# Two factors of the normalised input, T3 and T4, summed by accumulating transfers inside SBUF instead of VectorE

## The chip, the core and the metric
The kernel runs on one core of one Trainium2 chip. The metric is the device time of one launch in microseconds (us), as the median of several runs. The engines are TensorE (PE; its weight loads are PEld), VectorE (DVE), ScalarE (ACT), GpSimd (POOL) and SyncE (SP). SP and POOL also start transfers: SP through hardware queues, POOL through a software queue, which alone is used here for transfers that add to what lies at their target.

## The reference
A decoder trunk of two layers on 512 tokens of width 1024. Each layer is a gated feed-forward, a mixer, and a second gated feed-forward:

```
x = x + 0.5 * swiglu(rms_norm(x, ffn1_norm[l]), ffn1_w_gate[l], ffn1_w_up[l], ffn1_w_down[l])
x = x + mixer_l(rms_norm(x, mix_norm[l]))
x = x + 0.5 * swiglu(rms_norm(x, ffn2_norm[l]), ffn2_w_gate[l], ffn2_w_up[l], ffn2_w_down[l])

def rms_norm(x, g):
    y = x * rsqrt(mean(x * x, axis=-1) + 1e-6)
    return y * g
def swiglu(x, w_gate, w_up, w_down):
    return (silu(x @ w_gate) * (x @ w_up)) @ w_down
```
All inputs are float32; the hidden width is 2816.

## The kernel before, in words
`x` stays in SBUF, as eight tiles of 128 features by 512 tokens. The feed-forward `ffn` is called four times: first and second feed-forward of both layers, with a mixer between the first and the second call and another between the third and the fourth. Its matrix products use a scheme of seven products for a 2x2 block product. The normalised input is cut into four blocks: b11 and b12 are the first 512 features for the first and the last 256 tokens, b21 and b22 the same of the last 512 features. Its right factors are

- B11 = b11, B21 = b21, N22 = -b22,
- T1 = b12 - b11, N2 = T1 - b22, T3 = b22 - b12, T4 = b11 - b21 + T3 (written before as -(N2) - b21).

Every factor and every weight chunk is split into a high part, by a cast on ScalarE (L87), and a residue, by a subtraction on VectorE (L88); each product then takes three matmuls (high by high, high by residue, residue by high). The order of the products is fixed by hand (`staggered`): P5 and P1 of the first unit, then P6, P2, P7, then P5 of the next unit, P3, P1 of the next, P4. Their right factors are P5: T1, P1: B11, P6: N2, P2: B21, P7: T3, P3: N22, P4: T4.

A call begins with a stage of its own. The first pair of gate and up columns is computed from the input before its norm is known, by four `quarter`s of 24 matmuls of 512 columns each; the norm's sums (`norm`) are put in among them. While TensorE works on these, the normalised blocks `xn` are made on VectorE (L379) and the seven factors are built from them in the order of the code: B11, T1, N2, B21, T3, N22, T4. T1, N2 and T4 are made one after the other in the half `t1` of a tile `hz`, T3 in its other half `t3`. There is one buffer for `hz`: the next hidden tile of that name is first written at L460 and has to wait until everything in the old one has been read. The quarters' four PSUM banks are read at L455 and L458 (a product with R), L456 (SiLU on ScalarE) and L460 to L464. The PSUM pool has six banks: four for the quarters, two for X and Y of the first unit, so P2's bank Z comes free when a quarter's bank has been read. P1 and then P6, P7 and P4 write bank X in turn: P6 waits until ScalarE has copied P1's result away (`x1`, L482), P7 until it has copied P6's (`x2`, L482).

Weight chunks come by SP's transfers into `sto`, `ar` and `a`; the sums of weights that the scheme needs are made by accumulating transfers that POOL starts (L124). A scheduler sets each engine's order when the kernel is built, from the order of the code and the dependences; an engine works through its own list in order.

Of the kernel before, what the change touches and what calls it, by code (L numbers as in the profile page):

```python
# [13 lines left out]
ALU = mybir.AluOpType  # L14
# [27 lines left out]
def trunk(ctx: ExitStack, tc: tile.TileContext, a, out):  # L42
# [12 lines left out]
    nc = tc.nc  # L55
# [8 lines left out]
    def bank(tag="bank", bufs=None):  # L64
        return pp.tile([P, 512], F32, tag=tag, name=tag, bufs=bufs)
# [20 lines left out]
    def split(raw, hi, lo):  # L86
        nc.scalar.copy(hi, raw)  # L87
        nc.vector.tensor_sub(lo, raw, hi.bitcast(F32))  # L88
# [22 lines left out]
    class Seven(Chunk):  # L111
# [11 lines left out]
        def add(self, tag, q):  # L123
            nc.gpsimd.dma_start(out=self.unit[tag], in_=self.srcs[q], accum_op=ALU.add)  # L124
# [42 lines left out]
    for l in range(2):  # L167
        for f in ("ffn1", "ffn2"):
# [21 lines left out]
            for kind, p in what:  # L190
                if kind == "gu":
                    units.append(seven([gu[p, q] for q in range(4)], CH, turn))
                else:
                    gi, e = p
# [11 lines left out]
    def weights(ahead=3, fetched=6):  # L206
        i = used[0]
        used[0] += 1
        while len(ready) < min(i + ahead, len(chunks)):
            while (loaded[0] < min(max(len(ready) + 1, i + fetched), len(chunks))  # L210
                   and chunks[loaded[0]].turn <= now[0]):
                chunks[loaded[0]].load()
                loaded[0] += 1
            ready.append(chunks[len(ready)].halves())
        return ready[i]

    def mm3(ps, wh, wl, ah, al, start, stop):
        nc.tensor.matmul(ps, wh, ah, start=start, stop=False)  # L218
        nc.tensor.matmul(ps, wh, al, start=False, stop=False)  # L219
        nc.tensor.matmul(ps, wl, ah, start=False, stop=stop)  # L220
# [98 lines left out]
    def norm_columns():  # L319
        ps = held()  # L320
        for sq in Norm.late:
            nc.vector.tensor_add(Norm.acc, Norm.acc, sq)
        Norm.late.clear()
        token_sums(ps, Norm.acc)
        v = sp.tile([P, NT], F32, tag="nv", name="nv")
        nc.vector.tensor_scalar(v, ps[:, 0:2 * NT:2], 1.0 / D, EPS, ALU.mult, ALU.add)
        return rsqrt(v, NT, "n")

    def norm_rows(r):
        rb = tp.tile([P, NT, P], F32, tag="sq", name="rb")  # L330
        nc.vector.tensor_copy(rb, r.unsqueeze(2).broadcast_to([P, NT, P]))
        ps = held()
        for i in range(NT):
            nc.tensor.matmul(ps[:, i * P:(i + 1) * P], rb[:, i, :], ident, start=True, stop=True)
        R = tp.tile([P, T], F32, tag="R", name="R", bufs=1)
        nc.scalar.copy(R, ps)
        return R, ps


    def ffn(l, f, which, after, first=False):  # L340
        what, order = plans[l, f]
        with ExitStack() as es:
# [6 lines left out]
            def eight():  # L349
                return fp.tile([P, 8, HT], F32, tag="hz", name="hz")  # L350
# [4 lines left out]
            banks = [bank() for _ in range(4)]  # L355

            def quarter(outs, k0, start, stop, between=None):
                hi, lo = weights()
                for e, ps in enumerate(outs):
                    if e and between:  # L360
                        between()
                    for i in range(4):
                        s = slice((4 * e + i) * P, (4 * e + i + 1) * P)
                        mm3(ps, hi[:, s], lo[:, s], *xs[k0 + i], start and i == 0, stop and i == 3)
# [3 lines left out]
            norm = lambda: rows.extend(norm_rows(norm_columns()))  # L368
            quarter(banks[2:4], 0, True, False, None if first else norm)
            if first:  # L370
                norm()
            R, Rp = rows
            with tc.tile_pool(name="np", bufs=1) as np_:
                xn = [np_.tile([P, 4, T], F32, tag=f"xn{e}", name=f"xn{e}") for e in range(2)]

                def normal(e):
                    for i in range(4):
                        k = 4 * e + i
                        nc.vector.scalar_tensor_tensor(xn[e][:, i], x[k], gains[:, which, k:k + 1], R if e else Rp,  # L379
                                                       ALU.mult, ALU.mult)  # L380

                def factor(b, v, sign=1.0):
                    hi, lo = fac[b][:, 0], fac[b][:, 1]
                    if sign > 0:
                        split(v, hi, lo)
                    else:
                        nc.scalar.mul(hi, v, -1.0)
                        nc.vector.scalar_tensor_tensor(lo, v, -1.0, hi.bitcast(F32), ALU.mult, ALU.subtract)

                normal(0)  # L390
                b11, b12 = xn[0][:, :, :HT], xn[0][:, :, HT:]
                b21, b22 = xn[1][:, :, :HT], xn[1][:, :, HT:]
                factor("B11", b11)
                hz = eight()
                t1, t3 = hz[:, :4], hz[:, 4:]
                nc.vector.tensor_sub(t1, b12, b11)
                factor("T1", t1)
                normal(1)
                nc.vector.tensor_sub(t1, t1, b22)
                factor("N2", t1)  # L400
                factor("B21", b21)
                nc.vector.tensor_sub(t3, b22, b12)
                factor("T3", t3)
                factor("N22", b22, -1.0)
                nc.vector.scalar_tensor_tensor(t1, t1, -1.0, b21, ALU.mult, ALU.subtract)
                factor("T4", t1)
            quarter(banks[0:2], 4, False, True)
            quarter(banks[2:4], 4, False, True)


# [21 lines left out]
            B12, N22, B11, T1, N2, T3, B21, T4 = range(8)  # L432
# [502 lines left out]
    def odd_mixer(after):  # L935
        with tc.tile_pool(name="op", bufs=1) as op:
# [31 lines left out]
            for m in range(NK):  # L968
# [3 lines left out]
                after(m)  # L972

    ffn(0, "ffn1", 0, lambda m: norm_in(m, 1), True)
    even_mixer(lambda m: norm_in(m, 2))
    ffn(0, "ffn2", 2, lambda m: norm_in(m, 3))
    ffn(1, "ffn1", 3, lambda m: norm_in(m, 4))
    odd_mixer(lambda m: norm_in(m, 5))
    ffn(1, "ffn2", 5, store)
# [71 lines left out]
```

## Time and profile before
| | |
|---|---|
| median of 3 runs | 1764.47 us (1763.59 to 1764.65) |
| the profiled execution: own time | 1768.79 us |
| its span in the trace | 1767.0 us |
| mean granted clock of TensorE, as a share of 2.4 GHz | 0.985 |
| busy share PE, DVE, ACT, POOL | 96%, 75%, 51%, 18% |

The span is the time from the first to the last instruction in the trace; the execution's own time also holds what lies around it. Start times in the rows count from the span's start. The four calls' first stages lie at about 33 to 62, 580 to 604, 920 to 946 and 1440 to 1469 us.

### The profile page before, as it was taken

How to read it: one execution, taken by the hardware profiler on the slowest of the kernel's cores; microseconds unless marked ns; L12 is line 12 of the kernel's file. 1: busy time of each engine (PE TensorE's matmuls, PEld its weight loads, DVE VectorE, ACT ScalarE, POOL GpSimd, SP SyncE). 2: the span in 40 equal slices, each digit the busy share in tenths (PEclk: the TensorE clock that was granted, in tenths of full speed). 3: DMA queues.
4: the chain of work that ended last, by engine and by line, in shares of the span. 5: the costliest groups of instructions: out<-in, count | busy, mean ns of one | idle time of the engine just before them, and what ended most of it. 6: DMA issues, size and time to landing. Idle time of an engine off the chain costs nothing.

```text
span 1767.0 us, 31319 instructions
## 1 busy us (share of the span) xinstructions
PE 1697.0 (96%) x12642; PEld 1594.4 (90%) x12642; DVE 1328.1 (75%) x1891; ACT 906.9 (51%) x1300; POOL 312.0 (18%) x359
## 2 busy tenths in 40 slices
PE   7899999999999799999998999999999989999998
PEld 5799999978888799999988999999788879999998
DVE  6877786877896977677798777868755677867866
ACT  5654554564654554564556545545322345645553
POOL 2111111224202111111121111112100111111111
PEclk9999999998999899999999999999999999999999
DMA  6689888740015498889776899897322248988986
GB/s 215 157 209 215 216 211 212 165 142 24 19 42 173 106 214 218 213 206 217 173 194 153 208 219 223 207 212 164 108 96 96 96 133 194 222 216 209 218 210 138
DMA packets 89185, 303.19 MB, mean 172 GB/s; under 512 B 10704, under 2 KB 11472, under 8 KB 89040
## 3 DMA queue, kind: packets, MB, share of 16 engines
q0 software_dynamic: 36864, 130.04, 42.1%
q1 hardware_dynamic: 50512, 169.89, 27.2%
q8 instruction: 99, 1.62, 0.4%
q10 hardware_dynamic: 1664, 1.26, 0.2%
q14 instruction: 46, 0.38, 0.1%
HBM read 299.06 MB, written 2.10 MB: 170 GB/s over the span
## 4 chain that ended last, share of the span: by engine, by line
PE 80%; DVE 10%; issue 3%; ACT 3%; DMA 3%; POOL 1%; SPq 0%; ACTq 0%; DVEq 0%; POOLq 0%
PE bank L476 61%; PE bank L218 5%; PE bank L219 5%; PE bank L220 5%; DMA sto<-in_ffn_w_gu 2%; DVE wlo L88 2%; ACT whi L87 1%; DVE xn L379 1%; DVE xs L242 1%; DVE fT L88 1%; DVE fB L88 1%; PE bank L882 0%; PE held L218 0%; PE held L219 0%; PE held L220 0%
## 5 line engine op out<-in xcount | busy, mean ns | idle before, releaser
L476 PE MATMUL bank<-hh,whi 128*128 128x256 f32 x2464 | 429.9, 278 | 7.3 <-ACT whi L87 3.9
L476 PEld LDWEIGHTS bank<-hh,whi 128*128 128x128 f32 x2464 | 374.3, 188 | 10.4 <-ACT whi L87 4.9
L476 PE MATMUL bank<-fT,whi 128*128 128x256 f32 x1920 | 337.8, 279 | 8.5 <-ACT whi L87 2.9
L476 PE MATMUL bank<-hh,wlo 128*128 128x256 f32 x1232 | 341.5, 278 | 4.1 <-DVE wlo L88 4.1
L87 ACT CAST whi<-sto 128x1024 fp32r<-128x1024 f32 (+1 forms) x192 | 196.1, 1023 | 263.7 <-PE bank L476 164.4
L88 DVE TENSOR_TENSOR wlo<-sto,whi 128x1024 fp32r<-128x1024 f32 (+1 forms) x192 | 228.8, 1192 | 107.4 <-ACT whi L87 106.1
L476 PEld LDWEIGHTS bank<-fT,whi 128*128 128x128 f32 x1920 | 292.1, 189 | 11.2 <-ACT whi L87 3.5
L476 PE MATMUL bank<-fT,wlo 128*128 128x256 f32 x960 | 266.7, 278 | 0.0
L476 PE MATMUL bank<-fN,whi 128*128 128x256 f32 x1280 | 237.5, 288 | 14.4 <-ACT x L482 9.5
L476 PEld LDWEIGHTS bank<-hh,wlo 128*128 128x128 f32 x1232 | 231.0, 188 | 4.9 <-DVE wlo L88 4.9
L476 PE MATMUL bank<-fB,whi 128*128 128x256 f32 x1280 | 231.3, 280 | 4.2 <-DVE t L455 4.1
L476 PEld LDWEIGHTS bank<-fN,whi 128*128 128x128 f32 x1280 | 199.3, 193 | 25.3 <-ACT x L482 13.6
L87 ACT CAST whi<-a 128x1024 fp32r<-128x1024 f32 (+1 forms) x128 | 131.3, 1026 | 144.4 <-PE bank L476 88.1
L476 PEld LDWEIGHTS bank<-fB,whi 128*128 128x128 f32 x1280 | 197.8, 190 | 4.9 <-DVE t L455 4.9
L124 POOL DMA_DIRECT2D sto<-in_ffn_w_gu x120 | 104.6, 871 | 517.3 <-DVE wlo L88 294.9
L88 DVE TENSOR_TENSOR wlo<-a,whi 128x1024 fp32r<-128x1024 f32 (+1 forms) x128 | 152.3, 1190 | 53.3 <-ACT whi L87 53.0
L88 DVE TENSOR_TENSOR wlo<-ar,whi 128x1024 fp32r<-128x1024 f32 (+1 forms) x128 | 152.3, 1190 | 49.1 <-ACT whi L87 48.8
L87 ACT CAST whi<-ar 128x1024 fp32r<-128x1024 f32 (+1 forms) x128 | 130.9, 1022 | 112.2 <-PE bank L476 55.6
L476 PE MATMUL bank<-fN,wlo 128*128 128x256 f32 x640 | 181.3, 283 | 6.2 <-DVE wlo L88 6.2
L476 PE MATMUL bank<-fB,wlo 128*128 128x256 f32 x640 | 178.7, 279 | 5.5 <-DVE wlo L88 5.5
L476 PEld LDWEIGHTS bank<-fT,wlo 128*128 128x128 f32 x960 | 181.3, 189 | 0.0
L219 PE MATMUL bank<-xs,whi 128*128 128x512 f32 x392 | 154.9, 395 | 1.8 <-DVE xs L242 1.6
(242 smaller groups left out, 2877.9 us busy)
## 6 DMA issues: line engine op xcount, KB each, us to landing
sto<-in_ffn_w_gu POOLq DMA_DIRECT2D x120, 512.0 KB, 7.4
a<-in_ffn_w_gu SPq DMA_DIRECT2D x80, 512.0 KB, 6.5
sto<-in_ffn_w_down POOLq DMA_DIRECT2D x48, 512.0 KB, 7.7
sto<-in_ffn_w_gu SPq DMA_DIRECT2D x40, 512.0 KB, 4.2
ar<-in_ffn_w_gu SPq DMA_DIRECT2D x40, 512.0 KB, 5.4
ar<-in_ffn_w_gu POOLq DMA_DIRECT2D x40, 512.0 KB, 5.4
a<-in_ffn_w_down SPq DMA_DIRECT2D x32, 512.0 KB, 6.0
raw<-in_c_w_in SPq DMA_DIRECT2D x24, 512.0 KB, 3.4
```

The source lines that it names most:

```text
L87: nc.scalar.copy(hi, raw)
L88: nc.vector.tensor_sub(lo, raw, hi.bitcast(F32))
L124: nc.gpsimd.dma_start(out=self.unit[tag], in_=self.srcs[q], accum_op=ALU.add)
L218: nc.tensor.matmul(ps, wh, ah, start=start, stop=False)
L219: nc.tensor.matmul(ps, wh, al, start=False, stop=False)
L220: nc.tensor.matmul(ps, wl, ah, start=False, stop=stop)
L242: nc.vector.scalar_tensor_tensor(xl, x[k], g, xh.bitcast(F32), ALU.mult, ALU.subtract)
L379: nc.vector.scalar_tensor_tensor(xn[e][:, i], x[k], gains[:, which, k:k + 1], R if e else Rp, ALU.mult, ALU.mult)
L476: nc.tensor.matmul(o, w_[:, s], a_, start=fresh and e == 0 and k == 0 and i == 0, stop=last and i == 2, skip_group_check=True)
```

## The change
T3 and T4 are no longer made by VectorE. ScalarE writes -b12 into `t3` and turns the sign of b21 in place. Three sums are then made by accumulating transfers from SBUF into SBUF, started by POOL: t3 += b22, b21 += b11, b21 += t3. Each sum is cut into two transfers of half the blocks, 128 partitions by 2x256 float32 (256 KB, in runs of 1 KB). T3 is split from `t3` as before, T4 now from the place of b21. In the first call only, the third quarter is issued ahead of the fourth with the norm inside it; before, the norm stood ahead of both in that call. Behind this piece the lines of the changed kernel have numbers that are 9 higher (L455 is L464 there, L460 is L469, L482 is L491); the adds are L405.

```diff
             quarter(banks[2:4], 0, True, False, None if first else norm)
             if first:
-                norm()
+                quarter(banks[0:2], 4, False, True, norm)
...
                 factor("N2", t1)
                 factor("B21", b21)
-                nc.vector.tensor_sub(t3, b22, b12)
+
+                def add(o, i):
+                    for e in range(0, 4, 2):
+                        nc.gpsimd.dma_start(out=o[:, e:e + 2], in_=i[:, e:e + 2], accum_op=ALU.add)
+
+                nc.scalar.mul(t3, b12, -1.0)
+                add(t3, b22)
+                nc.scalar.mul(b21, b21, -1.0)
+                add(b21, b11)
+                add(b21, t3)
+                factor("N22", b22, -1.0)
                 factor("T3", t3)
-                factor("N22", b22, -1.0)
-                nc.vector.scalar_tensor_tensor(t1, t1, -1.0, b21, ALU.mult, ALU.subtract)
-                factor("T4", t1)
-            quarter(banks[0:2], 4, False, True)
+                factor("T4", b21)
+            if not first:
+                quarter(banks[0:2], 4, False, True)
             quarter(banks[2:4], 4, False, True)
```

The first place is VectorE's list in the third call, from B11's residue to the first write of the next `hz`. In these rows fB, fN, fT are the factors' buffers by the first letter of their names, `sto`, `a` and `ar` weight chunks. Before:

```order
L88 TENSOR_TENSOR fB_10249<-xn_10350,fB_10249 128x1024
L402 TENSOR_TENSOR hz<-xn_10350,xn_10349 128x1024
L88 TENSOR_TENSOR fN_10248<-hz,fN_10248 128x1024
L388 SCALAR_TENSOR_TENSOR fN_10251<-xn_10350,fN_10251 128x1024
L88 TENSOR_TENSOR fT_10250<-hz,fT_10250 128x1024
L405 SCALAR_TENSOR_TENSOR hz<-hz,xn_10350 128x1024
L455 TENSOR_TENSOR t<-bank,R 128x512
L458 TENSOR_TENSOR v<-bank,R 128x512
L88 TENSOR_TENSOR fT_10252<-hz,fT_10252 128x1024
L88 TENSOR_TENSOR wlo<-sto,whi 128x1024
L460 TENSOR_TENSOR hz<-v,t 128x256
```

And in the changed kernel:

```order
L88 TENSOR_TENSOR fB_10261<-xn_10362,fB_10261 128x1024
L388 SCALAR_TENSOR_TENSOR fN_10263<-xn_10362,fN_10263 128x1024
L88 TENSOR_TENSOR fN_10260<-hz,fN_10260 128x1024
L464 TENSOR_TENSOR t<-bank,R 128x512
L88 TENSOR_TENSOR fT_10262<-hz,fT_10262 128x1024
L467 TENSOR_TENSOR v<-bank,R 128x512
L88 TENSOR_TENSOR wlo<-sto,whi 128x1024
L88 TENSOR_TENSOR wlo<-a_10397,whi 128x1024
L88 TENSOR_TENSOR wlo<-ar,whi 128x1024
L469 TENSOR_TENSOR hz<-v,t 128x256
L470 TENSOR_TENSOR hz<-v,t 128x256
L88 TENSOR_TENSOR fT_10264<-xn_10362,fT_10264 128x1024
```

L402 and L405 are gone, T4's residue has moved behind L469, and two more weight splits stand ahead of L469.

The second place is ScalarE's list in the third call, from N2's cast to the copy of bank X that P7 waits for (the second COPY). In the changed kernel:

```order
L87 CAST fN_10260<-hz 128x1024
L409 ACTIVATE xn_10362<-xn_10362 128x4x256
L87 CAST fT_10262<-hz 128x1024
L87 CAST whi<-a_10397 128x1024
L465 ACT_TABLE_LOAD
L465 ACTIVATE t<-t 128x512
L491 COPY x_10537<-bank 128x512
L87 CAST whi<-ar 128x1024
L87 CAST fT_10264<-xn_10362 128x1024
L87 CAST whi<-sto 128x1024
L491 COPY x_10569<-bank 128x512
```

Before, T4's cast stood behind the copy of P1's result and ahead of the quarters' SiLU, and nothing of T4 stood between the SiLU and the second copy; now T4's cast and a weight cast stand right ahead of it, behind a sign change (L409) early in the list.

The third place is POOL's list, in the third and then in the fourth call:

```order
L124 DMA sto<-in_ffn_w_gu 128x1024 x2
L405 DMA hz<-xn_10362 128x2x256 x2
L124 DMA ar<-in_ffn_w_gu 128x1024
L405 DMA xn_10362<-xn_10361 128x2x256 x2
L405 DMA xn_10362<-hz 128x2x256 x2
L124 DMA sto<-in_ffn_w_gu 128x1024 x3
```

```order
L405 DMA hz<-xn_15515 128x2x256 x2
L124 DMA sto<-in_ffn_w_gu 128x1024
L405 DMA xn_15515<-xn_15514 128x2x256 x2
L405 DMA xn_15515<-hz 128x2x256
L124 DMA ar<-in_ffn_w_gu 128x1024
L405 DMA xn_15515<-hz 128x2x256
L124 DMA sto<-in_ffn_w_gu 128x1024 x3
```

In both the adds stand among the weight accumulates of the first units, which were the only ones there before; in the fourth call one of these stands between the two halves of the last add.

## Rows read from the trace of the kernel before
**Rows 1.** The page: busy time, share of the span, instructions; then the chain by engine
```profile
PE 1697.0 (96%) x12642; PEld 1594.4 (90%) x12642; DVE 1328.1 (75%) x1891; ACT 906.9 (51%) x1300; POOL 312.0 (18%) x359
...
PE 80%; DVE 10%; issue 3%; ACT 3%; DMA 3%; POOL 1%; SPq 0%; ACTq 0%; DVEq 0%; POOLq 0%
```

**Rows 2.** Windows, third call: PE, PEld, DVE, ACT, POOL busy, PEclk, DMA share, GB/s
```profile
930.00:945.00 15.00, 10.13 (x67) 9.42 (x66) 15.00 (x21) 8.89 (x11) 0.87 (x1) 0.77 0.45 79
```

**Rows 3.** Timeline of PE: start, us, instruction [idle before <-releaser]; fT at P7's start
```profile
52.24 0.79 PE L476 MATMUL bank<-fB,whi 128*128 128x256 f32 x2 [3.63 <-DVE t L455]
...
62.02 0.39 PE L476 MATMUL bank<-fT,whi 128*128 128x256 f32 x2
...
603.49 0.39 PE L476 MATMUL bank<-fT,whi 128*128 128x256 f32 x2
...
939.50 0.58 PE L476 MATMUL bank<-fN,wlo 128*128 128x256 f32 x1 [2.07 <-DVE wlo L88]
...
946.24 0.39 PE L476 MATMUL bank<-fT,whi 128*128 128x256 f32 x2
...
1468.65 0.39 PE L476 MATMUL bank<-fT,whi 128*128 128x256 f32 x2
```

**Rows 4.** Timeline of DVE, third call
```profile
934.76 1.22 DVE L405 SCALAR_TENSOR_TENSOR hz<-hz,xn 128x1024 f32<-128x1024 f32 x1
...
937.09 1.22 DVE L88 TENSOR_TENSOR fT<-hz,fT 128x1024 fp32r<-128x1024 f32 x1
938.23 1.22 DVE L88 TENSOR_TENSOR wlo<-sto,whi 128x1024 fp32r<-128x1024 f32 x1
939.37 0.42 DVE L460 TENSOR_TENSOR hz<-v,t 128x256 f32<-128x256 f32 x1
...
945.52 1.23 DVE L88 TENSOR_TENSOR wlo<-sto,whi 128x1024 fp32r<-128x1024 f32 x1 [0.25 <-ACT whi L87]
...
948.36 2.16 DVE L88 TENSOR_TENSOR hh<-hz,hh 128x1024 fp32r<-128x1024 f32 x3 [1.28 <-ACT hh L87]
```

**Rows 5.** Timeline of ACT: N2's cast in the four calls, and the copy before P7
```profile
45.39 1.04 ACT L87 CAST fN<-hz 128x1024 fp32r<-128x1024 f32 x1
...
585.77 1.05 ACT L87 CAST fN<-hz 128x1024 fp32r<-128x1024 f32 x1
...
929.78 1.05 ACT L87 CAST fN<-hz 128x1024 fp32r<-128x1024 f32 x1
...
943.95 0.59 ACT L482 COPY x<-bank 128x512 f32<-128x512 f32 x1 [1.37 <-PE bank L476]
...
1446.58 1.05 ACT L87 CAST fN<-hz 128x1024 fp32r<-128x1024 f32 x1 [0.26 <-DVE hz L399]
```

**Rows 6.** Timeline of POOL: two accumulates issued one after the other
```profile
612.22 0.85 POOL L124 DMA_DIRECT2D ar<-in_ffn_w_gu  x1 [7.57 <-issue]
613.57 0.88 POOL L124 DMA_DIRECT2D sto<-in_ffn_w_gu  x1 [0.49 <-issue]
```

**Rows 7.** Accumulates, KB, us to landing: 916 to 955 us, whole program; then the software queue
```profile
sto<-in_ffn_w_gu POOLq DMA_DIRECT2D x3, 512.0 KB, 5.4
ar<-in_ffn_w_gu POOLq DMA_DIRECT2D x2, 512.0 KB, 5.5
...
sto<-in_ffn_w_gu POOLq DMA_DIRECT2D x120, 512.0 KB, 7.4
...
q0 software_dynamic: 36864, 130.04, 42.1%
```

**Rows 8.** Windows of PE alone: us, PE busy (matmuls), PEclk, DMA share, GB/s
```profile
34.00:40.00 6.00, 6.00 (x28) 1.00 0.23 45
...
52.00:56.00 4.00, 1.68 (x6) 0.51 0.00 0
...
596.00:600.00 4.00, 4.00 (x21) 0.50 0.60 93
604.00:608.00 4.00, 4.00 (x37) 1.00 0.67 114
```

## The prediction
> **What bounds the kernel now.** I read the busy shares and the chain of waits first [rows 1]: TensorE is busy 96% of the span and carries 80% of the chain, VectorE 10%. VectorE's 75% is an average; what an operation off it is worth depends on the stage. So I looked at the stage the change touches, the start of each feed-forward call, in the third one: between 930 and 945 us VectorE is busy 15.00 of 15 us, ScalarE 8.89, the DMA engines 45%, and TensorE only 10.13 at a granted clock of 0.77 [rows 2]. VectorE bounds this stage. The timeline of TensorE says how [rows 3]: it stands until a quarter's bank is read (L455) and until the residue of P6's weights is split (2.07 us for `wlo`). After the longer stop, 3.63 us in the first call, the clock is granted at half, 1.2 GHz, then at full, 2.4 GHz [rows 8]. The reader should see that a microsecond on VectorE before 939.5 is worth a microsecond of TensorE here, four times in the program, and that P7 starts (946.24) only when P6 and P2 are through.
>
> **What the change takes away.** Per call two VectorE operations go, L402 and L405. Operations of 128x1024 follow each other at 1.14 us (937.09, 938.23, 939.37 [rows 4]), so 2.28 us. The new order also puts T4's split behind the splits of the weights, a third 1.14: P6's residue is split 3.42 us earlier, at 934.81 instead of 938.23. In the first call it is less, because the third quarter now runs ahead of the norm: the norm's sums stand behind 12 more 512-wide matmuls of 0.214 us (28 in 6.00 us [rows 8]), 2.57 us later, while one weight split of 1.14 no longer stands between; 1.4 late, so 2.0 gained. If nothing else bound, 3 x 3.42 + 2.0 = 12.2 us would be the whole gain.
>
> **What it adds on ScalarE.** Two sign changes of 128x1024, priced as the neighbouring casts, 1.05 us each [rows 5]. ScalarE is busy 8.89 of 15 us, and 2.1 us fit in its waits; if they didn't, they would be paid four times, 8.4 us.
>
> **What it adds on GpSimd's queue.** Six accumulating transfers per call, 256 KB each. An issue holds the engine 0.85 to 0.88 us and two in a row start 1.35 apart (612.22, 613.57 [rows 6]). The 24 transfers move 6.3 MB beside the 130.04 MB that this queue carries [rows 7]; with DMA engines 45% busy I cost the bytes at nothing as load, but not as latency.
>
> **The latency is the open price.** The trace has no transfer inside SBUF. The nearest row is a 512 KB accumulate from HBM in the same stage, 5.4 us from issue to landing (x3; 5.5 for the other two); over the whole program it is 7.4 [rows 7]. Upper bound: half the bytes land no sooner, 5.4. For the lower bound I take the bytes off: the software queue's packets took 42.1% of 16 x 1767.0 us over 36864 packets, 0.323 us each; such a transfer has one 4 KB row per partition, 128 packets on 16 engines, 8 each, 2.6 us; with none of that left it is 2.8. I take half of the bytes off, 5.4 - 1.3 = **4.1 us**, since half the data moves but in runs of 1 KB instead of 4.
> The Trainium skill, page "DMA: Bandwidth & Descriptors", section "Anatomy of one DMA — SWDGE (gpsimd) path", speaks for less: about 2.0 us plus bytes over 436 GB/s, an estimate of 2.6 us for 256 KB; with it the sum would be rival A's. By that rule the 512 KB accumulate would land in 3.2 us; this trace shows 5.4, so here it does not agree.
>
> **The new path to P7.** T4 is ready when three things have followed each other: the sign of B21 (L409), the first pair of its adds, the second pair. From the end of L409: the first add's second half is issued 1.35 after the first and lands at 1.35 + 4.1 = 5.45; the half behind it is issued then and lands at 9.55; 2 x 0.5 for GpSimd to take up a wait (its issues stood 0.49 idle even with nothing to wait for [rows 6]) and 0.9 for rings shared with weights (about half of 7.4 - 5.4) make 11.45. In the fourth call the last half stands behind a 512 KB weight accumulate, 8 packets per engine: +2.6, 14.0.
> What queues behind it: on ScalarE T4's cast now stands ahead of a weight cast and of the copy of bank X (`x2`, L491) that lets P7 write that bank, so P7 waits for 1.05 + 1.05 + 0.59 = 2.7 more. On VectorE, L469 writes the next hidden tile over T3, which the last add still reads; behind L469 stands all of VectorE's work. On GpSimd the next weight accumulates wait until the last add is issued, about 939, where they are issued today.
>
> P7's start is N2's cast [rows 5] + 1.05 + 1.05 + 11.45 + 2.7 = + 16.2:
> - third call: 929.78 + 16.2 = 946.0, now 946.24: -0.2
> - second: 585.77 + 16.2 = 602.0, now 603.49: -1.5
> - first: 45.39 + 1.4 + 16.2 = 63.0, now 62.02: +1.0
> - fourth: 1446.58 + 16.2 + 2.6 + 1.05 (T3's cast is ahead of L409) = 1466.4, now 1468.65: -2.2
>
> So P7 starts about where it does. But TensorE gets there sooner: P6's residue is ready at 934.81 + 1.22 = 936.0, 48 matmuls at 0.108 us (37 in 4.00 us [rows 8]) end at 941.2, and it stands 4.8 us. That is longer than the 3.63 us after which the clock was at half. I expect half the clock for P7's 24 matmuls: 0.190 us each (21 in 4.00 us) instead of 0.108, **+2.0** each call. P7 ends at +1.8, +0.5, +3.0, -0.2: **+5.1 us**.
>
> VectorE reaches L469 at 939.37 - 2.28 - 1.14 + 2.28 (two more weight splits ahead of it) = 938.2 and waits for the landing at 929.78 + 2.1 + 11.45 = 943.3: 5.1 us idle. Against this stand the 2.28 it no longer does and the waits of 0.25 and 1.28 it had [rows 4]: 1.3 us late, four times, **+5.2 us**, where every engine behind it draws on its splits.
>
> **The sum.** The 12.2 brings nothing while P7 waits for the adds; 5.1 + 5.2 = +10.3 us on the profiled execution's own 1768.79 is 1779.1. That execution lies 4.3 us (0.24%) above the median of the runs. On the median, 1764.47 + 10.3 = **1775**. If P7's delay and VectorE's overlap entirely, +5.2: 1769.7.
>
> **Rivals.** All hang on the landing time L of a 256 KB add; the chain is 2L + 3.25.
> - *A, faster.* L is 2.8 or less: the chain is 8.85, P7 starts at 943.4, TensorE stands 2.2 us, less than 3.63, and the clock stays; VectorE waits 2.4 us at L469, less than the 3.81 it has over. Then the gain on VectorE remains, up to 12.2: 1752. For it: no HBM is involved, and the DMA engines are at 45%. Against it: 5.4 for the nearest row.
> - *B, no change.* L is near 3.4, the break-even: the chain is 1.4 shorter, P7's term falls by 4 x 1.4 to -0.5 and VectorE's to nothing. 1764. Above 3.4 the change costs time.
> - *C, slower still.* L is the full 5.4, since 1 KB runs undo the smaller size: chain +2.6, 4 x 2.6 = +10.4 where both engines shift together, twice that where they add: 1785 to 1796.
> - *D.* A packet costs 0.323 us whatever its size; with 1 KB runs there are 256 for half the bytes, 16 per engine, and the chain doubles to about 23: +46, 1821.
> That the change does not do what it says is excluded: the new order has the adds in place of L402 and L405 in all four calls.
>
> **How the numbers follow.** Forecast (L 3.8 to 4.7, its two terms added or overlapping: 1768 to 1784) 0.49, A 0.17, B 0.16, C 0.15, D 0.03. The range leaves out A and D: from B's 1762 to the middle of C, 1791. A measurement of this kernel tells 0.2% (3.5 us) from no change: A is faster, 0.17; B the same, 0.16; the others slower, 0.67. A and B hang on a latency that no row shows, so the odds of a gain are kept at one in six.
>
> **What would show it.** In the changed kernel's profile: the adds' median landing near 4.1 us; P7's first matmul in the third call near 946, with an idle time of some 5 us before it that is put down to the copy of x, and a granted clock near 0.5 in the 2 us behind it; VectorE idle some 5 us ahead of L469; the sign changes at 1.05 us; about 9 us less busy time on VectorE (8 x 1.14). The forecast is wrong if the adds land in under 3.4 us, if the clock stays at full through P7, or if VectorE's wait at L469 is under 3.8 us.

## The result, and the profile after

The changed kernel takes 1822.92 us (median of 4 runs, 1818.86 to 1829.91) against 1764.03 before: ratio 1.0349, 95% interval 1.0324 to 1.0375. The forecast, 1775 with a range up to 1791, had the sign; of the loss of about 59 us it had 10. The profiled execution took 1829.91 us, with a span of 1828.1: 61.1 more than before.

The page of the changed kernel, busy shares and chain, beside [rows 1]:

```profile
PE 1706.6 (93%) x12642; PEld 1604.0 (88%) x12642; DVE 1318.2 (72%) x1883; ACT 914.0 (50%) x1308; POOL 341.2 (19%) x383
...
PE 74%; DVE 8%; issue 6%; DMA 6%; ACT 4%; POOL 2%; SPq 0%; ACTq 0%; POOLq 0%; DVEq 0%
```

VectorE did what was asked: 9.9 us less busy (9.1 forecast), and its share of the chain fell. DMA rose from 3% to 6% of it. TensorE is busy 9.6 us longer with the same matmuls. The groups by line show where it stands (busy, mean ns, idle before and what ended it; fT is the buffer of T1, T3 and T4, whi a weight's high part):

```profile
L485 PE MATMUL bank<-fT,whi 128*128 128x256 f32 x1920 | 352.4, 286 | 66.2 <-ACT x L491 56.9 <-ACT whi L87 4.5 <-DVE fT L88 2.5
```

The same group before:

```profile
L476 PE MATMUL bank<-fT,whi 128*128 128x256 f32 x1920 | 337.8, 279 | 8.5 <-ACT whi L87 2.9 <-issue 2.2 <-ACT x L482 1.7
```

It stood 8.5 us in all, 1.7 of them for ScalarE's copy of bank X. That copy is now waited for 56.9 us. So the 61.1 us are 55.2 of this wait and 9.6 of slower matmuls, less 3.7 saved elsewhere. The timeline of PE places the wait: it is ahead of the first matmul of P7, in the first unit of each call and, shorter, in the second unit (99.56 is that of the first call).

```profile
72.58 0.80 PE L485 MATMUL bank<-fT,whi 128*128 128x256 f32 x2 [11.10 <-ACT x L491]
99.56 0.70 PE L485 MATMUL bank<-fT,whi 128*128 128x256 f32 x2 [4.28 <-ACT x L491]
...
626.18 0.80 PE L485 MATMUL bank<-fT,whi 128*128 128x256 f32 x2 [11.69 <-ACT x L491]
...
983.50 0.80 PE L485 MATMUL bank<-fT,whi 128*128 128x256 f32 x2 [10.40 <-ACT x L491]
...
1516.12 0.80 PE L485 MATMUL bank<-fT,whi 128*128 128x256 f32 x2 [9.90 <-ACT x L491]
```

The four first units stand 43.1 us; the second units' P7 (4.28, 2.42, 2.71 and 4.11) another 13.5. What holds the copy is in ScalarE's timeline of the third call:

```profile
958.32 1.05 ACT L409 ACTIVATE xn<-xn 128x1024 f32<-128x1024 f32 x1
...
980.97 1.04 ACT L87 CAST fT<-xn 128x1024 fp32r<-128x1024 f32 x1 [14.82 <-DMA xn<-hz]
981.92 1.04 ACT L87 CAST whi<-sto 128x1024 fp32r<-128x1024 f32 x1
982.87 0.58 ACT L491 COPY x<-bank 128x512 f32<-128x512 f32 x1
```

T4's cast stands in the list ahead of the copy and waits 14.82 us for the last add. From the end of the sign change of B21 (959.4) to that cast it is **21.6 us, where the prediction had 11.45**. GpSimd's timeline shows the chain:

```profile
957.62 1.39 POOL L124 DMA_DIRECT2D ar<-in_ffn_w_gu  x1
961.10 1.20 POOL L405 DMA_DIRECT2D xn<-xn  x1 [2.08 <-issue]
965.80 1.21 POOL L405 DMA_DIRECT2D xn<-xn  x1 [3.50 <-issue]
973.01 1.20 POOL L405 DMA_DIRECT2D xn<-hz  x1 [6.00 <-DMA xn<-xn]
977.10 1.21 POOL L405 DMA_DIRECT2D xn<-hz  x1 [2.89 <-issue]
977.83 1.42 POOL L124 DMA_DIRECT2D sto<-in_ffn_w_gu  x1
```

The two halves of an add start 4.70 and 4.09 us apart, not 1.35 as two weight accumulates do [rows 6], and before the second halves here GpSimd waits for nothing that the profile shows. Nor does VectorE hold it: VectorE is idle from 967.4 to 981.0, while the last pair goes out 4.09 us apart. The landing is near the forecast at the median of the 24 adds (3.8 us for 4.1), but not in the second sum. The view of the adds' own line, and the second sum's transfers (KB each, median us to landing):

```profile
  DVE hz L469: 56.7, 4
...
DMA to landing us min/median/max: 3.7/3.8/8.0
```

```profile
xn<-xn POOLq DMA_DIRECT2D x8, 256.0 KB, 5.2
```

In all twelve pairs the second half starts about 0.3 us after the first has landed, while the weight accumulate right behind a pair starts 0.7 us after it (977.10, 977.83). The first of these views has VectorE's waits ahead of L469: 56.7 us in four calls, for instance

```profile
980.99 0.43 DVE L469 TENSOR_TENSOR hz<-v,t 128x256 f32<-128x256 f32 x1 [13.59 <-DMA xn<-hz]
```

After P7's stop TensorE's clock is granted at half, 1.2 GHz (0.50 from 984 to 987), and then in full. Windows of PE alone (us, busy and matmuls, granted clock, DMA share, GB/s): 24 matmuls take 4.50 us at a mean of 0.59, and then 25 take 2.60.

```profile
983.50:988.00 4.50, 4.50 (x24) 0.59 0.04 6
988.00:990.60 2.60, 2.60 (x25) 1.00 0.70 104
```

### The profile page after: what moved, and what is told of

The parts are those of the page before. It is cut to its first block, busy times and chain, and to the rows that moved or that the text cites. A ratio compares the mean times of both kernels' runs of the same rounds, so it can differ in the third digit from the quotient of the medians.

```text
span 1828.1 us, 31385 instructions
## 1 busy us (share of the span) xinstructions
PE 1706.6 (93%) x12642; PEld 1604.0 (88%) x12642; DVE 1318.2 (72%) x1883; ACT 914.0 (50%) x1308; POOL 341.2 (19%) x383
## 4 chain that ended last, share of the span: by engine, by line
PE 74%; DVE 8%; issue 6%; DMA 6%; ACT 4%; POOL 2%; SPq 0%; ACTq 0%; POOLq 0%; DVEq 0%
PE bank L485 56%; PE bank L218 5%; PE bank L219 5%; PE bank L220 5%; DMA sto<-in_ffn_w_gu 2%; DVE wlo L88 2%; DMA ar<-in_ffn_w_gu 2%; ACT whi L87 1%; DMA sto<-in_ffn_w_down 1%; DMA xn<-hz 1%; POOL xn L405 1%; DVE xn L379 1%; DVE xs L242 1%; PE bank L891 0%; PE held L218 0%
## 5 line engine op out<-in xcount | busy, mean ns | idle before, releaser
L485 PE MATMUL bank<-hh,whi 128*128 128x256 f32 x2464 | 427.5, 277 | 7.3 <-ACT whi L87 4.6
L485 PE MATMUL bank<-fT,whi 128*128 128x256 f32 x1920 | 352.4, 286 | 66.2 <-ACT x L491 56.9
L485 PEld LDWEIGHTS bank<-hh,whi 128*128 128x128 f32 x2464 | 372.5, 188 | 10.5 <-ACT whi L87 5.6
L485 PEld LDWEIGHTS bank<-fT,whi 128*128 128x128 f32 x1920 | 303.0, 195 | 71.0 <-ACT x L491 59.5
L485 PE MATMUL bank<-hh,wlo 128*128 128x256 f32 x1232 | 340.7, 277 | 5.4 <-DVE wlo L88 5.4
L485 PE MATMUL bank<-fT,wlo 128*128 128x256 f32 x960 | 272.8, 284 | 0.0
L485 PE MATMUL bank<-fN,whi 128*128 128x256 f32 x1280 | 238.4, 288 | 11.4 <-ACT x L491 8.9
L485 PEld LDWEIGHTS bank<-hh,wlo 128*128 128x128 f32 x1232 | 231.3, 188 | 6.5 <-DVE wlo L88 6.2
L485 PE MATMUL bank<-fB,whi 128*128 128x256 f32 x1280 | 231.1, 280 | 4.4 <-ACT whi L87 4.3
L485 PEld LDWEIGHTS bank<-fN,whi 128*128 128x128 f32 x1280 | 199.4, 193 | 21.7 <-ACT x L491 12.9
L485 PEld LDWEIGHTS bank<-fB,whi 128*128 128x128 f32 x1280 | 197.2, 190 | 5.0 <-ACT whi L87 5.0
L485 PEld LDWEIGHTS bank<-fT,wlo 128*128 128x128 f32 x960 | 187.0, 195 | 0.0
L485 PE MATMUL bank<-fB,wlo 128*128 128x256 f32 x640 | 178.8, 279 | 4.3 <-DVE wlo L88 4.3
L485 PE MATMUL bank<-fN,wlo 128*128 128x256 f32 x640 | 181.3, 283 | 1.6 <-DVE wlo L88 1.6
```

The costliest lines, as they stand in the source:

```text
L485: nc.tensor.matmul(o, w_[:, s], a_, start=fresh and e == 0 and k == 0 and i == 0, stop=last and i == 2, skip_group_check=True)
```

## The experiments

All kernels below compute the whole reference. Edits move lines: the product's matmul (L485 here) and the copy of bank X (L491) have other numbers in them. Ratios are to the kernel before on the same chip; a point is 1% of its time, 17.6 us.

### Are the halves held by their pieces? lay2k, quarters, lay4k, beforelay

Theory: a 256 KB half in 1 KB runs is 256 pieces (a piece is one contiguous run in one partition), and the queue doesn't take a second one until the first is through. Rival: the landing is what is slow, or the load. `lay2k` stores the normalised blocks so that each is contiguous; a half is then 128 pieces of 2 KB.

```diff
-                xn = [np_.tile([P, 4, T], F32, tag=f"xn{e}", name=f"xn{e}") for e in range(2)]
+                xn = [np_.tile([P, 2, 4, HT], F32, tag=f"xn{e}", name=f"xn{e}") for e in range(2)]
...
-                b11, b12 = xn[0][:, :, :HT], xn[0][:, :, HT:]
-                b21, b22 = xn[1][:, :, :HT], xn[1][:, :, HT:]
+                b11, b12 = xn[0][:, 0], xn[0][:, 1]
+                b21, b22 = xn[1][:, 0], xn[1][:, 1]
...
+                    o, i = (v.rearrange("p e t -> p (e t)") for v in (o, i))
+                    for e in range(0, 4 * HT, 2 * HT):
+                        nc.gpsimd.dma_start(out=o[:, e:e + 2 * HT], in_=i[:, e:e + 2 * HT], accum_op=ALU.add)
```

> The changed kernel with the normalised tile laid out so that each block is contiguous in a partition: the same six transfers of 256 KB per call in the same order, now in 128 pieces of 2 KB instead of 256 of 1 KB. Theory Q (the software queue holds only so many pieces: 384 outstanding are seen in the trace of the change, 512 never, so a second half of 256 pieces has to wait until the first has landed): the second half starts about 1.35 us after the first instead of 4.1, from L409's end to the last landing 11 to 13 us instead of 21.6, VectorE waits 4 to 6 us at the first write of hz instead of 13.6 to 14.9, time 1770 to 1785. Rival S (an accumulate inside SBUF is only started when the one before has landed, whatever its pieces): spacing stays near 4, chain 19 to 22, time 1810 to 1830.

Measured: 1.0185 [1.0168, 1.0202], 1797.28 us. GpSimd's timeline, third call:

```profile
945.43 1.78 POOL L407 DMA_DIRECT2D xn<-xn  x2 [2.89 <-ACT xn L411]
950.26 0.86 POOL L407 DMA_DIRECT2D xn<-hz  x1 [3.05 <-DMA xn<-xn]
951.74 0.86 POOL L407 DMA_DIRECT2D xn<-hz  x1 [0.63 <-issue]
```

The pair of the second sum goes out in a row, that of the third 1.48 apart, and 1.64 points (29 us) are gone. The landing of the first sum fell only from 3.8 to 3.3. ScalarE's timeline, third call, from the sign change to T4's cast:

```profile
943.96 1.06 ACT L411 ACTIVATE xn<-xn 128x1024 f32<-128x1024 f32 x1
...
959.03 1.04 ACT L87 CAST fT<-xn 128x1024 fp32r<-128x1024 f32 x1 [8.76 <-DMA xn<-hz]
```

That is 14.0 us, where 11 to 13 were expected: the last sum's transfers, now beside each other and beside weights, took 6.7 us to land (median). The time, too, is above the expected 1770 to 1785. The order of every engine's list is that of the changed kernel, so the run shows what the chain costs: over the four calls it is 57.0 us (13.5, 13.9, 14.0, 15.6) instead of 85.3 (21.4, 22.9, 21.6, 19.5), so 28.3 us of chain are worth 29 us of time.

`quarters` keeps the runs of 1 KB and the old layout, and cuts each sum into four transfers of 128 pieces:

```diff
-                    for e in range(0, 4, 2):
-                        nc.gpsimd.dma_start(out=o[:, e:e + 2], in_=i[:, e:e + 2], accum_op=ALU.add)
+                    for e in range(4):
+                        nc.gpsimd.dma_start(out=o[:, e], in_=i[:, e], accum_op=ALU.add)
```

> The changed kernel with each sum in four transfers of 128 KB, 128 pieces of 1 KB each: the same pieces and bytes, twelve transfers per call. Theory Q: three can be outstanding, so they start about 1.35 us apart and the fourth waits for the first to land; chain 12 to 15 us from L409's end, time 1772 to 1795. Rival S: eight landings of 3.3 us or more one after the other, 26 us or more, 1835 or more. Rival H (GpSimd needs 4.1 us to write the pieces of a 256-piece transfer, so 2 us for 128): spacing 2 us, chain about 20, near 1815.

Measured: 1.0162 [1.0139, 1.0184], 1793.1 us, in the theory's range. Twice the transfers, the same bytes in the same runs, and 1.87 points less: runs of 1 KB are not what is slow, nor is the number of transfers. (On VectorE and ScalarE three or four operations changed places as well.) GpSimd's timeline, first call:

```profile
48.66 2.76 POOL L405 DMA_DIRECT2D xn<-xn  x3 [2.86 <-ACT xn L409]
51.63 0.88 POOL L405 DMA_DIRECT2D xn<-xn  x1 [0.21 <-issue]
```

`lay4k` makes each sum one transfer of 128 pieces of 4 KB (`range(0, 4 * HT, 4 * HT)` in the layout of lay2k):

> The same layout, each sum as one transfer of 512 KB in 128 pieces of 4 KB: three transfers per call. Both theories: two landings in a row of about 5.4 each plus about 1 for the waits, 12 us from L409's end, time 1770 to 1785. If the time of a landing is set by the bytes and not by the start, it is as slow as lay2k or slower by up to 1.4 us per call; if a start costs more than half the bytes, it is faster than lay2k.

Measured: 1.0158 [1.0132, 1.0185], 1794.24 us, above the expected range and not told apart from the other two. `beforelay` is the kernel before with the layout alone:

> The kernel before with the new layout of the normalised tile alone: what the layout does by itself. 1764, within 3 us either way, if strided reads of 4 x 256 cost VectorE and ScalarE the same as contiguous ones; if lay2k and lay4k owe anything to the layout, it shows here.

Measured: 0.9994 [0.9982, 1.0006]. The layout costs and brings nothing by itself.

### GpSimd's list behind the adds: afterkeep, lay2kkeep

The adds also moved two weight accumulates, which the prediction's rows of GpSimd didn't reach. In the first call, from the last add on, the list of the changed kernel, with the second unit's `ar` behind the third unit's first `sto`:

```
L405 DMA xn<-hz x2
L124 DMA sto<-in_ffn_w_gu x3
L124 DMA ar<-in_ffn_w_gu
```

Before, it stood ahead of it (`sto` x2, `ar`, `sto` x3 in the same place). The trace of the changed kernel, GpSimd:

```profile
76.38 0.87 POOL L124 DMA_DIRECT2D sto<-in_ffn_w_gu  x1 [8.10 <-DVE hz L448]
83.90 0.86 POOL L124 DMA_DIRECT2D sto<-in_ffn_w_gu  x1 [6.65 <-DVE hz L500]
84.60 1.07 POOL L124 DMA_DIRECT2D ar<-in_ffn_w_gu  x1
```

That `ar` is for the second unit's own products (P7 among them) and lands 10.6 us later, behind the 512 KB of `sto`, which landed in 5.4. `afterkeep` is the changed kernel with one edge in the order per call (nothing is waited for, only the list changes):

```diff
+            if tag == "sto" and q == 3 and n == 2:
+                tc.add_manual_dep(r.ins, sums[self.turn, n - 1],
+                                  mybir.DependencyInfo(mybir.DependencyClass.NoSync, mybir.DependencyReason.DATA),
+                                  reason="order")
```

> The changed kernel, with one order edge per call on GpSimd's list: the first weight accumulate of the third unit (sto) again behind the sum of the second unit's weights for P7 (ar), as in the kernel before; the change had swapped the two. Nothing else moves on any engine. Theory R (of the 13 to 19 us that each call lost, the part that appears behind P7, 3 to 6 us, is the second unit's P7 waiting for this ar, which now stands behind an sto that has to wait for a buffer): 1823 falls to 1800 to 1812, and the second unit's P7 is no longer held by the cast of ar. Rival (that part comes from VectorE's backlog after its wait at the first write of hz): 1818 to 1826.

Measured: 1.0287 [1.0267, 1.0308], 1812.21 us; 0.62 points from the order of two transfers. The group of fT matmuls:

```profile
L495 PE MATMUL bank<-fT,whi 128*128 128x256 f32 x1920 | 348.0, 284 | 53.1 <-ACT x L501 44.1 <-ACT whi L87 4.3 <-DVE fT L88 2.5
```

12.8 us of the wait for the copy are gone, and no other engine's list has changed. `lay2kkeep` has the same edge on lay2k:

> lay2k (pieces of 2 KB, halves 1.35 us apart) with the same order edge. Theory R: 1797 falls by the same amount as the change itself, to 1775 to 1785; what is left is the wait of P7 and VectorE for the last landing. Rival: 1793 to 1800.

Measured: 1.0115 [1.0096, 1.0134], 1781.58 us: 0.70 points less than lay2k. The two causes add up: 1.64 and 0.70 of the 3.49 points.

### The waits at L469 and at the copy: afterin, afterinx, inplacex

`afterin` sums T3 in place over b12, so that L469 no longer writes over what an add reads:

```diff
-                nc.scalar.mul(t3, b12, -1.0)
-                add(t3, b22)
+                nc.scalar.mul(b12, b12, -1.0)
+                add(b12, b22)
...
-                add(b21, t3)
+                add(b21, b12)
...
-                factor("T3", t3)
+                factor("T3", b12)
```

> The changed kernel with T3 summed in place over b12 instead of in hz: VectorE no longer waits for the last add at the first write of hz; ScalarE's list (T4's cast ahead of the copy that P7 waits for), the pieces of 1 KB and the swapped ar stay. If the two waits add (as the prediction summed them), 1823 falls by about the part behind P7 that the order edge did not explain, to 1805 to 1815; if P7's wait alone sets the time and VectorE's overlaps with it, 1816 to 1824.

Measured: 1.0257 [1.0236, 1.0277], 1807.11 us, 0.92 points (16 us). The wait at L469 is gone, but VectorE then waits at T4's residue for its cast (44.9 us in all), so this doesn't price that wait by itself. By the timeline of PE the first units' P7 still wait 41.0 us (43.1), the second units' 1.0 (13.5). The gain is where afterkeep's is (41.2 and 2.8 there), and largely for the same reason: in the second, third and fourth call GpSimd's list has the second unit's `ar` ahead of the third unit's first `sto` again, without an edge. So the time lies in the range expected for waits that add, but the order changed with it, and the range decides nothing; beside afterkeep 0.30 points are left, with intervals that overlap. `afterinx` adds afterkeep's edge, and puts T4's cast behind the copy `x2` on ScalarE by another such edge:

```diff
+                if name == "x2" and "T4" in casts:
+                    tc.add_manual_dep(casts.pop("T4").ins, last.ins.name,
...
```

> afterin with the order edge on GpSimd's list, and T4's cast on ScalarE put behind the copy of P6's result, so that P7 no longer waits for the last add; the six transfers in 256 pieces of 1 KB each, one landing after the other, stay. If the price of the chain is only what waits for it, most of the 50 to 60 us goes though the chain is as long as before: 1760 to 1775. VectorE still meets T4's residue ahead of the hidden tile's splits, some 4 to 8 us after P7's start, which may keep a part. If instead the transfers cost by load, 1790 or more.

Measured: 1.0238 [1.0224, 1.0252], 1805.31 us: hardly less and far from the expected 1760 to 1775, though P7 of the third call no longer waits. The wait went on to P5 of the next unit; timelines of ScalarE and of PE:

```profile
969.28 1.04 ACT L87 CAST fT<-xn 128x1024 fp32r<-128x1024 f32 x1 [8.12 <-DMA xn<-xn]
970.24 1.04 ACT L87 CAST whi<-sto 128x1024 fp32r<-128x1024 f32 x1
```

```profile
971.33 0.74 PE L498 MATMUL bank<-fT,whi 128*128 128x256 f32 x2 [5.03 <-ACT whi L87]
```

The cast of P5's weight stands right behind T4's, which still waits for the adds. In the fourth call P7 itself still waits, for the copy behind the cast of an `ar` whose accumulate is queued between the halves of the last add; ScalarE, then PE:

```profile
1497.18 1.04 ACT L87 CAST whi<-ar 128x1024 fp32r<-128x1024 f32 x1 [12.12 <-DMA ar<-in_ffn_w_gu]
...
1500.23 0.79 PE L498 MATMUL bank<-fT,whi 128*128 128x256 f32 x2 [9.61 <-ACT x L504]
```

`inplacex` is afterinx with lay4k's layout and transfers, and T4's split written behind the quarters' results:

> afterinx with the contiguous layout and one transfer of 512 KB, 4 KB pieces, for each sum: chain of about 12 us, nothing of T4 on the way to P7 and no wait at hz. If the prediction's gain on VectorE (3.4 us per call ahead of P6's residue) is real, it is left over here: 1750 to 1758, faster than the kernel before. Rival: P7 is held by ScalarE's list otherwise, 1760 to 1766.

Measured: 1.0042 [1.0029, 1.0056], 1770.14 us. Of afterinx's 2.38 points 1.96 went with the pieces and T4's later place together; since the same bytes are moved here, afterinx's time isn't their load. The gain that was expected here (1750 to 1758) didn't come. The timeline of PE, third call: P5 of the first unit, P7, and P5 of the second.

```profile
926.42 0.40 PE L504 MATMUL bank<-fT,whi 128*128 128x256 f32 x2
...
942.80 0.40 PE L504 MATMUL bank<-fT,whi 128*128 128x256 f32 x2
...
946.45 0.51 PE L504 MATMUL bank<-fT,whi 128*128 128x256 f32 x2 [0.66 <-ACT whi L87]
...
948.90 0.39 PE L504 MATMUL bank<-fT,wlo 128*128 128x256 f32 x1 [1.95 <-DVE wlo L88]
```

From P5 to P7 it is 16.38 us; before 18.73 (927.51 to 946.24). Over four calls these stretches are 11.4 us shorter (1.4, 2.7, 2.4 and 5.0). So the gain of a shorter VectorE exists. It is then given back in P5 of the second unit, where the weight's cast again stands behind T4's.

### The weight sum behind the last add: finalc, final, finaln

`finalc` is inplacex with T4's cast put behind the next copy, that of P7's result:

> inplacex, with T4's cast moved further back on ScalarE, behind the copy of P7's result, and so its residue on VectorE too. If T4's wait ahead of the next product's weights was what cost 4 to 8 us behind P7, most of it goes: 1752 to 1760. If the late landing of the weight accumulate behind the last add was it, it stays at 1766 to 1772.

Measured: 1.0078 [1.0053, 1.0102], 0.36 points above inplacex and, at 1775.84 us, above both expected ranges. In the third call one stop of 4.97 us, ahead of P1 of the second unit, has taken the place of inplacex's short ones, and the matmuls behind it run at the slow pace (0.79 us for two, not 0.51; granted clock 0.50 from 953.4 to 956.0); that this is the whole difference wasn't tried. `final` puts the last add behind the `sto` accumulate it stood ahead of (`back` holds the last add of the call):

```diff
+            if tag == "sto" and q == 1 and n == 0:
+                for d in back:
+                    tc.add_manual_dep(d, r.ins.name,
...
```

> finalc, with the last add issued behind the weight accumulate (sto) that it stood ahead of on GpSimd's queue. If that accumulate's landing held the next product, this takes it away: 1748 to 1757, and 3 us or more under the kernel before, since the 3.4 us per call on P6's residue are then kept. Rival: what is gained comes from T4's cast alone, and it equals finalc within 2 us.

Measured: 0.9970 [0.9956, 0.9983], 1758.11 us (1748 to 1757 expected), 4.5 under the kernel before. These are 1.08 points between two kernels that differ, in each call, in the order of two transfers and in nothing else. GpSimd, ScalarE and PE of finalc, third call:

```profile
938.14 0.87 POOL L422 DMA_DIRECT2D xn<-xn  x1 [6.14 <-DMA xn<-xn]
938.77 1.15 POOL L125 DMA_DIRECT2D sto<-in_ffn_w_gu  x1
```

```profile
947.85 1.05 ACT L87 CAST whi<-sto 128x1024 fp32r<-128x1024 f32 x1 [5.79 <-DMA sto<-in_ffn_w_gu]
```

```profile
953.40 0.79 PE L504 MATMUL bank<-fB,whi 128*128 128x256 f32 x2 [4.97 <-ACT whi L87]
```

The accumulate, issued 0.6 us behind the add, is there 9.0 us later; in final it lands in 5.4, as before the change [rows 7]. In final it is issued first and its cast doesn't wait for it:

```profile
926.49 0.87 POOL L125 DMA_DIRECT2D sto<-in_ffn_w_gu  x1 [3.83 <-DVE wlo L88]
928.92 0.87 POOL L428 DMA_DIRECT2D xn<-xn  x1 [1.56 <-DMA xn<-xn]
```

```profile
933.59 1.05 ACT L87 CAST whi<-sto 128x1024 fp32r<-128x1024 f32 x1 [1.03 <-PE bank L512]
```

The group of fT matmuls in final stands 8.8 us, as before the change (8.5):

```profile
L512 PE MATMUL bank<-fT,whi 128*128 128x256 f32 x1920 | 338.5, 279 | 8.8 <-ACT x L518 2.7 <-DVE fT L88 2.6 <-issue 2.5
```

`finaln` is final with the norm where the kernel before has it:

> final with the norm of the first call back where the kernel before has it, ahead of the third and fourth quarter. If normonly's +2.5 us is a cost of that place by itself, final improves by about as much: ratio 0.9945 to 0.9965, 1753 to 1757. Rival: inside this kernel the move costs nothing, since T3 and T4 are off VectorE: ratio 0.9960 to 0.9980, as final.

Measured: 0.9963 [0.9951, 0.9975], 1753.82 us beside 1759.83 for the kernel before on that chip. It isn't told apart from final.

### Without transfers: late, latex, gp

`late` is the kernel before with only the order of the splits: T4 is written by VectorE over b21, and N22 and T4 are split behind the quarters' results.

```diff
-                factor("N22", b22, -1.0)
-                nc.vector.scalar_tensor_tensor(t1, t1, -1.0, b21, ALU.mult, ALU.subtract)
-                factor("T4", t1)
+                nc.vector.scalar_tensor_tensor(b21, t1, -1.0, b21, ALU.mult, ALU.subtract)
...
+            factor("T4", b21)
+            factor("N22", b22, -1.0)
```

> The kernel before, T3 and T4 by VectorE as there, but T4 written over b21 (so that hz is free early) and the splits of N22 and T4 traced behind the quarters' results, so that weight residues and the quarters' banks come first on VectorE. If VectorE bounds this stage as the prediction says (each us ahead of P6's residue is a us of TensorE), P6's residue comes 2 to 3 us earlier in each call and the time is 1752 to 1760. Rival (P7 is held by the copies on ScalarE anyway, or the postponed splits are paid behind P7): 1762 to 1768.

Measured: 0.9983 [0.9971, 0.9995]. `latex` keeps N22's split in its place and holds T4's behind the copy of P7's result:

> No transfers: T3 and T4 by VectorE as in the kernel before, T4 over b21, and only T4's split moved back behind the copy of P7's result. VectorE saves 1.14 us per call ahead of P6's residue where the adds save 3.4. If VectorE's time there is what counts: 1758 to 1762, behind final by some 5 us. Rival: the order alone brings what the adds bring, 1750 to 1756.

Measured: 0.9978 [0.9965, 0.9991]. The intervals of late, latex, final and finaln overlap: by the medians half to three quarters of what final and finaln gain is had without a transfer. `gp` gives both sums to GpSimd's own arithmetic:

```diff
-                nc.vector.tensor_sub(t3, b22, b12)
+                nc.gpsimd.tensor_sub(t3, b22, b12)
...
-                nc.vector.scalar_tensor_tensor(t1, t1, -1.0, b21, ALU.mult, ALU.subtract)
-                factor("T4", t1)
+                nc.gpsimd.tensor_add(t1, t1, b21)
+                factor("T4", t1, -1.0)
```

> The kernel before with the two operations of T3 and T4 done by GpSimd as ordinary sums over 128x1024 (N2 + b21, the sign in the split) instead of by transfers: VectorE is relieved of the same 2.28 us per call, no queue and no landing in the path. From GpSimd's 128x512 sums of 1.3 to 1.9 us, about 2.6 to 3.8 each. If the gain on VectorE is real, 1753 to 1762. Rival (GpSimd and VectorE slow each other down, or GpSimd's weight accumulates are late behind the sums): 1764 to 1775.

Measured: 1.0097 [1.0079, 1.0116]. GpSimd's timeline, third call, beside VectorE's 1.22 us for such an operation [rows 4]. The first is slower than the expected 2.6 to 3.8, and the time is above both ranges; how much of the 17 us these two operations cost, and how much the weight sums that changed places with them on GpSimd, wasn't separated.

```profile
927.88 5.50 POOL L402 TENSOR_TENSOR hz<-xn,xn 128x1024 f32<-128x1024 f32 x1 [7.76 <-DVE xn L379]
...
936.95 3.26 POOL L405 TENSOR_TENSOR hz<-hz,xn 128x1024 f32<-128x1024 f32 x1 [2.71 <-DVE fN L88]
```

### The norm's place: normonly

The kernel before with the first call's third quarter ahead of the norm, as in the change:

```diff
-                norm()
+                quarter(banks[0:2], 4, False, True, norm)
```

> The kernel before with the third quarter of the first call issued ahead of the norm, as in the change, and nothing else. The prediction took it as 1.4 us later in that call for the factors: 0 to +1.5 us. Rival: TensorE's wait behind the norm's sums was in the path, so that it gains 1 to 2 us.

Measured: 1.0014 [1.0003, 1.0025], 2.5 us with an interval of 0.5 to 4.4; the prediction's 1.4 us in this call lies in it.

## Why the prediction was wrong

**Right.** VectorE's shorter list (9.9 us less busy), the sign change (1.05), the landing at the median (3.8 for 4.1), the place of the loss (P7 behind the copy of X, T4's cast ahead of it; from that cast to P7 2.53 us for the 2.7), half the clock behind it (+1.9 for +2.0 in the third call) and that VectorE waits at L469, though 13.6 us and not 5.1. The bound of the gain is near too: 11.4 of the 12.2 us appear between P5 and P7 once nothing holds P7. The calls agree less than their sum: 1.4 for 2.0 in the first, then 2.7, 2.4 and 5.0 for 3.4 each.

**The step that failed** is "the first add's second half is issued 1.35 after the first". Those 1.35 us came from transfers of 128 pieces; the halves have 256. In the third call, from the end of the sign change: 1.7 to the first half's issue, 4.70 to the second's, 7.2 until the next add's first half, 4.09 to its second, 3.9 to T4's cast, 21.6. Against 11.45 that is 3.35 for the first pair, 4.09 for the second (whose last half the prediction let go as soon as the first pair was through), and 2.8 because one landing took 6.9 us, not 4.1. It is that of the second sum's second half, the slow one in every call (6.8, 8.0, 6.9 and 5.8). In that stretch, weights arrived on both queues; that they stretched it wasn't tried. The prediction had 16 packets per engine for a half, in rival D, as a price per packet only; it didn't ask how many the queue holds. D's 1821 is near the measured time by chance: its 16 packets would give a landing of some 8 us, and by its own 2L + 3.25 a chain of 19.2, not 23; of the 24 landings one took 8.0, and most of the delay stands between the transfers.

**The sum.** Over the four calls the chain is 85.3 us, where the prediction had 3 x 11.45 + 14.0 = 48.4: 36.9 more. Its two terms grow by about as much each, to about 42. Added they would be 84 us, more than was lost. "The sum" took them as added. The runs speak for overlap: in lay2k both waits shrink with the chain, and 28.3 us less of it are worth 29 us, not twice that; between afterkeep and lay2kkeep it is 28.8 for 30. So of the loss of 59 us about 42 is the chain, counted once, and about 11 (0.62 to 0.70 points) the part below; where the other 6 go isn't settled (for lay2kkeep the same count leaves 9). The trace has the first in another way: P7 of the first units starts 9.3, 9.7, 9.7 and 5.9 us later behind N2's cast than before, 34.5 in all, and its slower matmuls, about 4 x 1.9, make 42.

**A slip without a price here.** "48 matmuls at 0.108 us" took P6 and P2 at the full clock, and rival A counts on "less than 3.63, and the clock stays". The trace of the kernel before already has the clock at half in the third call behind stops of 2.30, 0.50 and 2.07 us (the row below, as in [rows 8]), and so has that of the changed kernel in P6 (0.50 from 965 to 968). P6 and P2 took 7.9 us there, not 5.2. So TensorE reached P7 later and stood 10.4 us for a chain that would have given 15; P7's start, which ScalarE set, didn't move by it.

```profile
939.50:943.00 3.50, 3.50 (x16) 0.50 0.41 54
```

**Missed** is the order of two weight accumulates in the second unit. "On GpSimd the next weight accumulates wait until the last add is issued, about 939, where they are issued today" was said of the time of issue; it looked at neither the order behind the adds nor at what a 512 KB transfer does to the one queued behind it. The same thing, at the first unit's last `sto`, is what finalc pays. So the 11.4 us saved between P5 and P7 stay away until neither a weight's cast stands behind T4's on ScalarE nor a weight's sum behind the last add on GpSimd. With both in order, a gain of 0.3 to 0.4% remains, 5 to 6 us, and the runs without transfers have 0.2%, with intervals that overlap; where the other half of 11.4 goes isn't settled.

## What to carry to other kernels

Before a sum goes from an engine to the software queue, count the pieces of each transfer against those of transfers that the trace shows going out in a row: a halved transfer in shorter runs may hold as many pieces as a whole one, and then halving buys no overlap. List what stands behind it, in the queue and on the engine that takes its result up, two units far, and put what is due sooner ahead of it. And ask how much of the gain is the reordering alone; here it was half or more of a small gain, for no transfer at all.

## What the runs showed of the hardware

The software queue let 128 and 256 pieces be outstanding together, and three transfers of 128, but in no place of these traces two of 256 or four of 128: of two with 256, the second was issued when the first had landed. That it holds 384 pieces and not 512 is inferred from this count; nothing between was tried. Issuing 256 pieces takes GpSimd 1.21 us; 128 take 0.86, or 1.1 to 1.4 right behind another issue.

Landing inside SBUF, by size (transfers: KB each, median us to landing), for the first sum, always in 128 pieces, of 1, 2 and 4 KB: quarters, lay2k, lay4k. The last sum, beside weights, took longer (6.3, 6.7 and 7.4).

```profile
hz<-xn POOLq DMA_DIRECT2D x16, 128.0 KB, 2.7
```

```profile
hz<-xn POOLq DMA_DIRECT2D x8, 256.0 KB, 3.3
```

```profile
hz<-xn POOLq DMA_DIRECT2D x4, 512.0 KB, 4.8
```

About 2 us and 0.7 per 128 KB, some 190 GB/s. The Trainium skill, page "DMA: Bandwidth & Descriptors", section "Anatomy of one DMA — SWDGE (gpsimd) path", gives 2.0 us plus bytes over 436 GB/s, an estimate of 2.3, 2.6 and 3.2 us: its fixed part agrees with these traces, its slope doesn't. Whether that is because these transfers add, or because they stay inside SBUF, wasn't separated.
